# Feed forward input products cut to 256 columns, with twelve kinds of chunk beginnings

## The chip, the cores and the metric

One core of one Trainium2 chip runs the program. The metric is the device time of one execution in microseconds (us); less is better. The time before is the median of three runs.

## What is computed

The reference is a decoder trunk of two layers over 256 positions and a width of 2048, in float32: first a recurrent layer (RG-LRU) with its feed forward part, then a sliding-window attention layer with its feed forward part. The change touches the first half of the two feed forward parts alone:

```python
def swiglu_ffn(x, g, w_in, w_out):
    h = rms_norm(x, g)
    gate, up = jnp.split(h @ w_in, 2, axis=-1)
    return x + (jax.nn.silu(gate) * up) @ w_out
```

Here `x` is 256 x 2048, `w_in` 2048 x 11264 and `w_out` 5632 x 2048. Inputs and outputs are float32.

## The kernel before, in words

**Numbers in two halves.** Every float32 operand is split into a high half (the value rounded to the product format) and a low half (the rest). A product is then high weights by high activations, high weights by low activations, and low weights by high activations. Activations of one tile of 128 features lie side by side in a tile `s` of 512 columns: columns 0 to 255 the high halves of the 256 positions, columns 256 to 511 the low halves. So one matmul of 512 columns with the high weights makes the first two of the three products, and one of 256 columns with the low weights makes the third. The first goes to all 512 columns of a PSUM bank, the second to columns 0 to 255; the two halves of the bank are added when it is drained (`pull`, L341: a copy by ScalarE, an add by VectorE).

**Chunks and groups.** Weights come as 705 jobs of 512 KB, each a chunk of 2 x 128 input features (`kt` or `k`) by 4 x 128 outputs (`f`). `stream` loads a chunk four jobs ahead on SyncE's queue, splits it three jobs ahead (`split`: a copy by ScalarE at L240 into `hi`, a subtraction by VectorE at L241 into `lo`; four buffers each), and then issues its products. A feed forward input group is eight chunks (`group`, with `nk` = 16) that add up into four PSUM banks; two groups take turns with the eight banks. There are 22 groups a layer, 44 in all. A chunk holds eight tiles, and a tile is a pair (k, f).

**What sets the order.** `ffn` gives each group an order, `(None, *self.ORDERS)[g % 8]`: by turns the plain one and the seven of the table `ORDERS`, whose entries are written as (f, k, p), where p is `h` (512 columns of the high weights), `l` (256 columns of the low weights), or `a` and `b` (the two halves of `h`). The plain order goes through `prod` (L272 and L274, one h and one l by turns), the others through `ordered` (L298). The first seven chunks of a group follow its order. The last chunk always goes through `prod`, which turns the pair round for the last k (L268 and L269). In an abl group all products go to columns 0 to 255 of the bank, and the bank is drained by a copy alone (`whole`); its last chunk runs in halves too (L263, L264, L266). Background work (activations, norms, attention) is put between the jobs and at the middle of a job (`half_tick`, `run_bg`) as long as ScalarE and VectorE have room by the estimates that the program keeps.

Of the kernel before, what the change touches and what calls it, by code (L numbers as in the profile page):

```python
# [17 lines left out]
P = 128  # L18
D = 2048
T = 256  # L20
DFF = 5632
ND = D // P
NH = DFF // P
# [25 lines left out]
class Trunk:  # L49
# [208 lines left out]
    def prod(self, ps, hi, lo, c, xs, first, last, one=False):  # L258
# [16 lines left out]

    ORDERS = {
        "hhll": [(f, k, p) for f in range(4) for p in "hl" for k in range(2)],
        "allh": [(f, k, p) for p in "hl" for f in range(4) for k in range(2)],  # L280
        "abl": [(f, k, p) for f in range(4) for k in range(2) for p in "abl"],
        "banks": [(f, k, p) for k in range(2) for p in "hl" for f in range(4)],
        "turns": [(f, k, p) for k in range(2) for f in range(4) for p in "hl"],
        "hllh": [(f, k, p) for f in range(4) for k, p in ((0, "h"), (0, "l"), (1, "l"), (1, "h"))],
        "pairs": [(f, k, p) for k in range(2) for g in range(2) for p in "hl" for f in (2 * g, 2 * g + 1)],
    }

    def ordered(self, order, ps, hi, lo, x2, first):
        mm = self.nc.tensor.matmul
        todo = self.ORDERS[order]  # L290
        begun = set() if first else set(range(4))
        for n, (f, k, p) in enumerate(todo):
            if 2 * n == len(todo):
                self.half_tick()
            w = (lo if p == "l" else hi)[:, k * 512 + f * P:k * 512 + f * P + P]
            c0, c1 = {"h": (0, 2 * T), "l": (0, T), "a": (0, T), "b": (T, 2 * T)}[p]
            o = ps[f][:, 0:c1 - c0]
            mm(o, w, x2[k][:, c0:c1], start=f not in begun, stop=False)  # L298
            begun.add(f)

    def group(self, src, nk, xs, done, last=False, one=False, order=None):

        st = {}
        for c in range(nk // 2):
            def mm(hi, lo, c=c):
                if c == 0:
                    st["ps"] = [self.bank() for _ in range(4)]
                x2 = [self.need(xs[2 * c + kt]) for kt in range(2)]
                if c == nk // 2 - 1:

                    for f in range(4):
                        if f == 2:
                            self.half_tick()
                        for kt in range(2):
                            k = 2 * c + kt
                            self.prod(st["ps"][f], hi, lo, kt * 512 + f * P, x2[kt], False, k == nk - 1, one)
                elif not self.started:
                    self.started = True
                    for kt in range(2):
                        for part in ((hi, None), (None, lo)):  # L320
                            for f in range(4):
                                self.prod(st["ps"][f], *part, kt * 512 + f * P, x2[kt], kt == 0, False, one)
                        if kt == 0:
                            self.half_tick()
                elif order:
                    self.ordered(order, st["ps"], hi, lo, x2, c == 0)
                else:
                    for f in range(4):
                        if f == 2:
                            self.half_tick()  # L330
                        for kt in range(2):
                            k = 2 * c + kt
                            self.prod(st["ps"][f], hi, lo, kt * 512 + f * P, x2[kt], k == 0, False, one)
                if last:
                    for q in x2:
                        self.free(q)
                if c == nk // 2 - 1:
                    done(st["ps"])
            self.jobs.append((src(c), mm))

    def pull(self, ps):  # L341

        t = self.t()
        o = self.half()
        self.a(t, ps[:, T:2 * T])
        self.tt(o, ps[:, 0:T], t, ALU.add)
        self.free_bank(ps)
        return o

    def whole(self, ps):  # L350

        o = self.half()
        self.a(o, ps[:, 0:T])
        self.free_bank(ps)
        return o

# [92 lines left out]
    def ffn(self, l, xs, r, gains, rn, out=None):  # L449
        hid = [Val() for _ in range(NH)]  # L450
        w = self.d[f"ffn_in{l}"]
        for g in range(NH // 2):
            order = (None, *self.ORDERS)[g % 8]

            def done(ps, g=g, one=order == "abl"):
                v = [self.whole(p) if one else self.pull(p) for p in ps]

                def task():
                    while not self.rv[r].ready:
                        yield 1  # L460
                    rs = self.rstd[r][:, 0:T]
                    for h in range(2):
                        ga, up = v[2 * h], v[2 * h + 1]
                        self.tt(ga, ga, rs, ALU.mult)
                        self.a(ga, ga, AF.Silu)
                        self.tt(up, up, rs, ALU.mult)
                        yield
                        self.tt(ga, ga, up, ALU.mult)
                        while not self.slots:
                            yield 1  # L470
                        s = self.slot()
                        self.split_act(s, ga)
                        self.free_half(ga)
                        self.free_half(up)
                        hid[2 * g + h].ap = s
                        hid[2 * g + h].ready = True
                        yield
                self.spawn(task())
            self.group(lambda c, g=g: w[g, c], ND, xs, done, g == NH // 2 - 1, order == "abl", order)
        self.project(self.d[f"ffn_out{l}"], NH, hid, gains, rn, out)  # L480


# [561 lines left out]
```

## Time and profile before

| | |
|---|---|
| median of the three runs | 2039.64 us (2039.63 to 2039.89) |
| the profiled execution | 2040.28 us |
| its span, first to last instruction | 2038.4 us |
| TensorE busy (matmuls) | 2027.7 us, 99% |
| VectorE busy | 1315.1 us, 65% |
| ScalarE busy | 1102.0 us, 54% |
| DMA | 376.10 MB, mean 185 GB/s |
| granted TensorE clock | 1.00 |

The page calls TensorE's matmuls PE and its weight loads PEld, VectorE DVE and ScalarE ACT. Every matmul instruction has a weight load of its own, and the loads run beside the matmuls before them. The ends of matmuls are modelled: one that is shown with 0.28 us is followed by the next some 0.12 us after its start. So the time of a matmul in a run is read from start to start, and where a row merges several of them (x8), its length is that from the first start to the last modelled end.

### The profile page before, as it was taken

What the parts mean: (1) busy time and instruction counts of PE and PEld (TensorE: products, weight loads), DVE (VectorE), ACT (ScalarE), POOL (GpSimd) and SP (SyncE); (2) the same over time, 40 slices, a digit from 0 to 9 for tenths busy, and PEclk for the clock granted to TensorE, in tenths of its full rate; (3) what the DMA queues carried; (4) which work ended last, traced back from release to release, by engine and by line L of the source; (5) the groups of instructions that cost most, each with busy time, mean ns of one, the idle gap of its engine ahead of it and who ended that gap; (6) DMA issues with size and microseconds to landing.
All of it is one profiled execution on the core that took longest, in us unless ns stands there. A gap on an engine that the chain in (4) does not pass through costs nothing.

```text
span 2038.4 us, 32783 instructions
## 1 busy us (share of the span) xinstructions
PE 2027.7 (99%) x12916; PEld 1827.5 (90%) x12916; DVE 1315.1 (65%) x2162; ACT 1102.0 (54%) x1737; POOL 0.2 (0%) x4
## 2 busy tenths in 40 slices
PE   8999999999999999999999999999999999999999
PEld 8999988988998898888898888899889889988899
DVE  8889867566656656545768776765665566554443
ACT  7689656445545544434556775654454454444342
POOL 0000000000000000000000000000000000000000
PEclk9999999999999999999999999999999999999999
DMA  7565555555555555555554335555556556556663
GB/s 258 182 192 182 192 187 186 193 189 186 193 190 189 191 189 187 190 191 186 188 185 145 119 118 167 186 187 191 191 186 196 187 187 195 187 187 200 200 197 125
DMA packets 104987, 376.10 MB, mean 185 GB/s; under 512 B 11648, under 2 KB 13824, under 8 KB 104832
## 3 DMA queue, kind: packets, MB, share of 16 engines
q1 hardware_dynamic: 104832, 374.01, 56.5%
q8 instruction: 101, 1.65, 0.3%
q14 instruction: 54, 0.44, 0.1%
HBM read 371.86 MB, written 2.10 MB: 183 GB/s over the span
## 4 chain that ended last, share of the span: by engine, by line
PE 98%; DVE 1%; DMA 0%; ACT 0%; issue 0%; SPq 0%; DVEq 0%
PE b L298 36%; PE b L272 28%; PE b L274 14%; PE b L264 4%; PE b L266 4%; PE b L263 4%; PE b L269 3%; PE b L268 1%; PE b L863 1%; DMA raw<-in_lru_in 0%; PE b L882 0%; PE b L929 0%; PE b L815 0%; PE b L817 0%; PE b L816 0%; DVE lo L241 0%
## 5 line engine op out<-in xcount | busy, mean ns | idle before, releaser
L241 DVE TENSOR_TENSOR lo<-raw,hi 128x1024 fp32r<-128x1024 f32 (+1 forms) x705 | 861.5, 1222 | 647.9 <-ACT hi L240 644.6
L240 ACT ACTIVATE hi<-raw 128x1024 fp32r<-128x1024 f32 (+1 forms) x705 | 745.3, 1058 | 821.1 <-PE b L272 336.9
L272 PE MATMUL b<-s,hi 128*128 128x512 f32 x2442 | 867.7, 395 | 0.0
L274 PE MATMUL b<-s,lo 128*128 128x256 f32 x2442 | 685.9, 281 | 0.0
L298 PE MATMUL b<-s,hi 128*128 128x512 f32 (+1 forms) x2464 | 655.2, 362 | 0.0
L272 PEld LDWEIGHTS b<-s,hi 128*128 128x128 f32 x2442 | 459.5, 188 | 95.9 <-issue 0.5
L274 PEld LDWEIGHTS b<-s,lo 128*128 128x128 f32 x2442 | 458.2, 188 | 8.9
L298 PE MATMUL b<-s,lo 128*128 128x256 f32 x2128 | 440.9, 279 | 0.0
L298 PEld LDWEIGHTS b<-s,hi 128*128 128x128 f32 x2464 | 403.5, 188 | 32.7
L298 PEld LDWEIGHTS b<-s,lo 128*128 128x128 f32 x2128 | 369.0, 188 | 43.0
L263 PE MATMUL b<-s,hi 128*128 128x256 f32 x800 | 224.9, 281 | 5.8 <-ACT hi L240 5.8
L264 PE MATMUL b<-s,hi 128*128 128x256 f32 x800 | 224.9, 281 | 0.0
L266 PE MATMUL b<-s,lo 128*128 128x256 f32 x800 | 223.6, 281 | 1.2 <-DVE lo L241 1.2
L263 PEld LDWEIGHTS b<-s,hi 128*128 128x128 f32 x800 | 151.5, 189 | 6.2 <-ACT hi L240 6.1
L266 PEld LDWEIGHTS b<-s,lo 128*128 128x128 f32 x800 | 150.2, 189 | 2.2 <-DVE lo L241 2.2
L264 PEld LDWEIGHTS b<-s,hi 128*128 128x128 f32 x800 | 151.5, 189 | 0.0
L104 ACT ACTIVATE t<-b 128x256 f32<-128x256 f32 x230 | 85.0, 380 | 39.4 <-PE b L269 33.5
L269 PE MATMUL b<-s,hi 128*128 128x512 f32 x230 | 90.3, 393 | 0.0
L113 DVE TENSOR_TENSOR h<-h,rstd 128x256 f32<-128x256 f32 x178 | 69.3, 418 | 0.2
L268 PE MATMUL b<-s,lo 128*128 128x256 f32 x230 | 64.2, 279 | 0.0
L113 DVE TENSOR_TENSOR h<-b,t 128x256 f32<-128x256 f32 x154 | 59.0, 417 | 0.2
L268 PEld LDWEIGHTS b<-s,lo 128*128 128x128 f32 x230 | 43.2, 188 | 10.0
(105 smaller groups left out, 993.3 us busy)
## 6 DMA issues: line engine op xcount, KB each, us to landing
raw<-in_ffn_in SPq DMA_DIRECT2D x352, 512.0 KB, 3.4
raw<-in_ffn_out SPq DMA_DIRECT2D x176, 512.0 KB, 3.5
raw<-in_lru_in SPq DMA_DIRECT2D x63, 512.0 KB, 3.9
raw<-in_lru_out SPq DMA_DIRECT2D x32, 512.0 KB, 3.5
raw<-in_w_q SPq DMA_DIRECT2D x32, 512.0 KB, 3.3
raw<-in_w_o SPq DMA_DIRECT2D x32, 512.0 KB, 3.4
raw<-in_gate SPq DMA_DIRECT2D x8, 512.0 KB, 3.5
raw<-in_kv SPq DMA_DIRECT2D x8, 512.0 KB, 3.3
```

Of the source, the lines that this page charges most:

```text
L104: self.nc.scalar.activation(out, in_, func, **kw)
L113: self.nc.vector.tensor_tensor(out, a, b, op)
L240: self.nc.scalar.activation(hi[:, q], raw[:, q], AF.Copy)
L241: self.nc.vector.tensor_tensor(lo[:, q], raw[:, q], hi[:, q].bitcast(F32), ALU.subtract)
L263: mm(ps[:, 0:T], hi[:, c:c + P], xs[:, 0:T], start=first, stop=False)
L264: mm(ps[:, 0:T], hi[:, c:c + P], xs[:, T:2 * T], start=False, stop=False)
L266: mm(ps[:, 0:T], lo[:, c:c + P], xs[:, 0:T], start=False, stop=last)
L268: mm(ps[:, 0:T], lo[:, c:c + P], xs[:, 0:T], start=False, stop=False)
L269: mm(ps[:, :], hi[:, c:c + P], xs[:, :], start=first, stop=True)
L272: mm(ps[:, :], hi[:, c:c + P], xs[:, :], start=first, stop=False)
L274: mm(ps[:, 0:T], lo[:, c:c + P], xs[:, 0:T], start=False, stop=False)
L298: mm(o, w, x2[k][:, c0:c1], start=f not in begun, stop=False)
```

## The change

The table of orders is gone. `ordered` now builds the order of a chunk from a beginning, a short word from the table `BEGIN`, chosen by layer, group and chunk. Each letter of the word takes a product of the next tile: `h` is 512 columns, `w` is columns 0 to 383 and `n` columns 384 to 511 of the tile begun with `w`, and `l` is the low weights of the first tile that has only its `h`. What is left of the chunk is done tile by tile in products of 256 columns (`a`, `b` and `l`; `a` and `b` both have the high weights). The first chunk of a group begins with four `h` and four `l` and does the other four tiles in 256 columns. The last chunk goes through `prod` as before. All groups now work this way, the plain ones too, and all banks have two halves, so `whole` is gone and every bank is drained by `pull`.

```diff
-    ORDERS = {
-        "hhll": [(f, k, p) for f in range(4) for p in "hl" for k in range(2)],
...
-    }
-    def ordered(self, order, ps, hi, lo, x2, first):
+    BEGIN = ["", "h", "hh", "hhh", "hhhh", "hhhhh", "hhhhhh", "hlh", "wn", "hlhh", "w", "hhlhh"]
+
+    def begins(self, l, g, c):
+        return self.BEGIN[(5 * c + 7 * g + 3 * l + g // 3) % len(self.BEGIN)]
+
+    def ordered(self, begin, ps, hi, lo, x2, first):
+
         mm = self.nc.tensor.matmul
...
+        cols = {"h": (0, 4), "a": (0, 2), "b": (2, 4), "l": (0, 2), "w": (0, 3), "n": (3, 4)}
+        tiles = [(k, f) for k in range(2) for f in range(4)]
+        todo, rest, t = [], [], iter(tiles)
+        if first:
+
+            todo = [(k, f, "h") for k, f in tiles[:4]] + [(k, f, "l") for k, f in tiles[:4]]
+            todo += [(k, f, p) for k, f in tiles[4:] for p in "abl"]
+        else:
+            done = {q: "" for q in tiles}
+            for p in begin:
+                if p == "n":
+                    q = next(q for q in tiles if done[q] == "w")
+                elif p == "l":
+                    q = next(q for q in tiles if done[q] == "h")
+                else:
+                    q = next(q for q in tiles if not done[q])
+                done[q] += p
+                todo.append((*q, p))
+            for q in tiles:
+                left = {"": "abl", "h": "l", "w": "nl", "wn": "l", "hl": ""}[done[q]]
+                todo += [(*q, p) for p in left]
...
+            c0, c1 = (P * q for q in cols[p])
+            mm(ps[f][:, c0:c1], w, x2[k][:, c0:c1], start=first and k == 0 and p == "h", stop=False)
...
-            order = (None, *self.ORDERS)[g % 8]
-
-            def done(ps, g=g, one=order == "abl"):
-                v = [self.whole(p) if one else self.pull(p) for p in ps]
+            def done(ps, g=g):
+                v = [self.pull(p) for p in ps]
...
-            self.group(lambda c, g=g: w[g, c], ND, xs, done, g == NH // 2 - 1, order == "abl", order)
+            self.group(lambda c, g=g: w[g, c], ND, xs, done, g == NH // 2 - 1,
+                       begins=lambda c, g=g: self.begins(l, g, c))
```

On TensorE the first feed forward group of layer 0 began like this (in a row: the line, the bank `b` that is written, the activations `s`, the weights `hi` or `lo`, and the columns):

```order
L272 MATMUL b_84<-s_2932,hi_75 128x512
L274 MATMUL b_84<-s_2932,lo_79 128x256
L272 MATMUL b_84<-s_2944,hi_75 128x512
L274 MATMUL b_84<-s_2944,lo_79 128x256
L272 MATMUL b_85<-s_2932,hi_75 128x512
L274 MATMUL b_85<-s_2932,lo_79 128x256
```

Its first chunk now reads as follows; `x2` marks the products `a` and `b` of one tile.

```order
L312 MATMUL b_83<-s_2932,hi_75 128x512
L312 MATMUL b_84<-s_2932,lo_79 128x256
L312 MATMUL b_85<-s_2932,lo_79 128x256
L312 MATMUL b_86<-s_2932,lo_79 128x256
L312 MATMUL b_83<-s_2932,lo_79 128x256
L312 MATMUL b_84<-s_2944,hi_75 128x256 x2
L312 MATMUL b_84<-s_2944,lo_79 128x256
L312 MATMUL b_85<-s_2944,hi_75 128x256 x2
L312 MATMUL b_85<-s_2944,lo_79 128x256
```

The row at the top is the last of four 512-wide products; behind it come sixteen 256-wide ones in a row where wide and narrow products took turns. The third chunk of the same group has the beginning `w`:

```order
L312 MATMUL b_84<-s_3104,hi_77 128x384
L312 MATMUL b_84<-s_3104,hi_77 128x128
L312 MATMUL b_84<-s_3104,lo_81 128x256
L312 MATMUL b_85<-s_3104,hi_77 128x256 x2
L312 MATMUL b_85<-s_3104,lo_81 128x256
```

Here one product of 512 columns became one of 384 and one of 128, and the other seven tiles are in products of 256 columns.

## Rows read from the trace of the kernel before

**Rows 1.** The page: engine totals, and the chain of waits by engine.

```profile
PE 2027.7 (99%) x12916; PEld 1827.5 (90%) x12916; DVE 1315.1 (65%) x2162; ACT 1102.0 (54%) x1737; POOL 0.2 (0%) x4
...
PE 98%; DVE 1%; DMA 0%; ACT 0%; issue 0%; SPq 0%; DVEq 0%
```

**Rows 2.** The page, costliest groups: busy, mean ns of one | idle before.

```profile
L241 DVE TENSOR_TENSOR lo<-raw,hi 128x1024 fp32r<-128x1024 f32 (+1 forms) x705 | 861.5, 1222 | 647.9 <-ACT hi L240 644.6
L240 ACT ACTIVATE hi<-raw 128x1024 fp32r<-128x1024 f32 (+1 forms) x705 | 745.3, 1058 | 821.1 <-PE b L272 336.9
```

**Rows 3.** Stretch of layer 0's input stage: length, PE busy, PEclk, DMA share, GB/s.

```profile
306.08:794.92 488.84, 488.84 (x3011) 1.00 0.58 190
```

**Rows 4.** The chain in layer 0's input stage, groups 1 to 6: start, us.

```profile
328.42 19.32 PE b L298 x112
350.50 19.28 PE b L298 x112
...
372.56 19.79 PE b L298 x168
395.17 19.37 PE b L298 x112
...
417.32 19.53 PE b L298 x112
...
439.65 19.32 PE b L298 x112
```

**Rows 5.** Timeline of TensorE, first chunks of the allh group: start, us, engine.

```profile
350.34 2.00 PE L298 MATMUL b<-s,hi 128*128 128x512 f32 x8
352.18 1.07 PE L298 MATMUL b<-s,lo 128*128 128x256 f32 x8
353.08 1.99 PE L298 MATMUL b<-s,hi 128*128 128x512 f32 x8
354.91 1.11 PE L298 MATMUL b<-s,lo 128*128 128x256 f32 x8
```

**Rows 6.** Two stretches in the projections of the first layer, 256-wide products only.

```profile
26.09:35.04 8.95, 8.95 (x81) 1.00 0.84 265
60.06:69.01 8.95, 8.95 (x79) 1.00 0.54 179
```

**Rows 7.** Timeline of TensorE in the hhll group.

```profile
328.72 0.39 PE L298 MATMUL b<-s,lo 128*128 128x256 f32 x2
328.95 0.62 PE L298 MATMUL b<-s,hi 128*128 128x512 f32 x2
329.40 0.40 PE L298 MATMUL b<-s,lo 128*128 128x256 f32 x2
329.64 0.62 PE L298 MATMUL b<-s,hi 128*128 128x512 f32 x2
```

**Rows 8.** Timeline of TensorE, from the hllh group to the pairs group.

```profile
461.57 0.62 PE L298 MATMUL b<-s,hi 128*128 128x512 f32 x2
462.03 0.39 PE L298 MATMUL b<-s,lo 128*128 128x256 f32 x2
462.25 0.62 PE L298 MATMUL b<-s,hi 128*128 128x512 f32 x2
```

**Rows 9.** Timeline of TensorE, first chunk of the banks group, behind abl.

```profile
395.01 1.09 PE L298 MATMUL b<-s,hi 128*128 128x512 f32 x4
395.94 0.62 PE L298 MATMUL b<-s,lo 128*128 128x256 f32 x4
396.39 1.07 PE L298 MATMUL b<-s,hi 128*128 128x512 f32 x4
397.31 0.63 PE L298 MATMUL b<-s,lo 128*128 128x256 f32 x4
397.78 1.09 PE L298 MATMUL b<-s,hi 128*128 128x512 f32 x4
```

**Rows 10.** The chain in the attention stage: 128-wide products.

```profile
1118.97 0.55 PE b L863 x5
```

More of the change, by code (lines that the diff above doesn't have):

```diff
@@ L274, in prod @@
                 mm(ps[:, 0:T], lo[:, c:c + P], xs[:, 0:T], start=False, stop=False)
-    ORDERS = {
-        "hhll": [(f, k, p) for f in range(4) for p in "hl" for k in range(2)],
[L280 to L285, printed above, removed]
-    }
@@ L288, in ordered @@
-    def ordered(self, order, ps, hi, lo, x2, first):
-        mm = self.nc.tensor.matmul
[L290 to L293, printed above, removed]
+    BEGIN = ["", "h", "hh", "hhh", "hhhh", "hhhhh", "hhhhhh", "hlh", "wn", "hlhh", "w", "hhlhh"]
+    def begins(self, l, g, c):
+        return self.BEGIN[(5 * c + 7 * g + 3 * l + g // 3) % len(self.BEGIN)]
+    def ordered(self, begin, ps, hi, lo, x2, first):
+        mm = self.nc.tensor.matmul
+        cols = {"h": (0, 4), "a": (0, 2), "b": (2, 4), "l": (0, 2), "w": (0, 3), "n": (3, 4)}
[18 more added lines that the diff above has]
+                todo += [(*q, p) for p in left]
+        for n, (k, f, p) in enumerate(todo):
+            if 2 * n == len(todo) - len(todo) % 2:
@@ L294, in ordered @@
                 self.half_tick()
             w = (lo if p == "l" else hi)[:, k * 512 + f * P:k * 512 + f * P + P]
[L296 to L301, printed above, removed]
+            c0, c1 = (P * q for q in cols[p])
+            mm(ps[f][:, c0:c1], w, x2[k][:, c0:c1], start=first and k == 0 and p == "h", stop=False)
@@ L303, in group @@
+    def group(self, src, nk, xs, done, last=False, one=False, begins=None):
         st = {}
@@ L324, in mm @@
                             self.half_tick()
-                elif order:
-                    self.ordered(order, st["ps"], hi, lo, x2, c == 0)
+                elif begins:
+                    self.ordered(begins(c), st["ps"], hi, lo, x2, c == 0)
                 else:
@@ L346, in pull @@
         self.tt(o, ps[:, 0:T], t, ALU.add)
[L347 to L353, printed above, removed]
         self.free_bank(ps)
```

## Prediction

> **What bounds the kernel now.** I read the page's totals first. TensorE is busy for 99% of the span, and the chain of waits that ended last is 98% TensorE [rows 1]. So the time is the sum of the start-to-start distances of the products, and nothing else is worth looking at as long as the other engines stay behind. Weights are split three chunks ahead: a chunk takes about 2.76 us on TensorE (19.32 / 7 [rows 4]), its two split instructions 1.06 us of ScalarE and 1.22 us of VectorE [rows 2].
>
> Next the stage that the change touches, as a stretch: 488.84 us in layer 0, all of it busy and at the full granted clock of 2.4 GHz [rows 3]; layer 1's stage repeats it, so 977.7 us together. Then the chain inside one of them. It merges the seven first chunks of each feed forward input group into one piece, and the six pieces here are the orders hhll, allh, abl, banks, turns and hllh [rows 4]; pairs, the next, repeats hllh's 19.32. All hold the same columns, 56 tiles of one 512-wide and one 256-wide product (in abl three of 256), and yet they take 19.28 to 19.79 us.
>
> The reason shows in the timeline, from start to start. In allh, eight wide products take 1.84 us in one chunk and 1.83 in the next, 0.229 each; but the eight narrow ones, shown from the first start to the modelled end of the last, take 1.07 us in the first chunk and 1.11 in the second [rows 5]. From start to start the first eight take 0.90 us, and 0.04 more makes 0.94 for the others. So **a run of 256-wide products has two paces**, about 0.113 and 0.118 us, called tight and loose from here on. A long run keeps its pace: the 168 of abl stand in 19.79 us, 0.1178 each, without a change [rows 4]. In the first layer's projections 8.95 us hold 81 products in one stretch (two of which began before it), 0.1133 each, and 79 in a later one of the same length and kind of products [rows 6]. So either pace can last for dozens of products; TensorE changes between them at a stall or behind wide products.
>
> Which pace follows can be read off. Behind a tight run, two wide products lead to a loose one and behind that loose run two lead to a tight one: in hhll the pairs of narrow ones alternate 0.23 and 0.24 us [rows 7]. Three behind a tight pair (the last of hllh and two of pairs) give a tight pair, 0.22 us [rows 8]. Four in banks go from loose to tight and from tight to loose, 0.45 and 0.47 us [rows 9], and the first four there follow the long loose run of abl. So of the counts modulo three, one keeps a tight pace, and behind a loose run two or four wide products bring it back.
>
> **The change, part by part.** First the counts, by the code. Outside the last chunk of each group there are 44 x 7 = 308 chunks. Before they hold 5,264 products; now 839 of 512 columns, 47 of 384, 47 of 128 and 5,620 of 256, together 6,553. The last chunks lose 48 products (the abl groups ran them in halves), so TensorE gets 1,241 products more for the same columns.
>
> Before, by [rows 4]: a layer has 22 groups, the eight orders in turn; the plain order alternates as turns does, so I give it the same 19.53. That is 3 x (19.53 + 19.32 + 19.28 + 19.79 + 19.37 + 19.53) + 2 x (19.32 + 19.32) = 427.7 us, for both layers 855.5.
>
> Now, if every narrow product is loose: 839 x 0.229 = 192.1; 5,620 x 0.1178 = 662.0; and 47 pairs of 384 and 128. No row has those widths in this stage. For 384 I take the middle of 0.118 and 0.229, 0.173. For 128 the bounds are 0.059 (half of a 256-wide product) and 0.118; the nearest row is five 128-wide products of the attention stage in 0.55 us, 0.110 [rows 10], and I take that. A pair is then 0.283 (bounds 0.177 and 0.347), all of them 13.3 us (8.3 to 16.3). The sum is 867.4, **+11.9 us**. If every one is tight, 5,620 x 0.1133 = 636.7 gives 842.1, **-13.4 us**. Last chunks: by the starts of the pieces an abl group lasts 395.17 - 372.56 = 22.61 us, so its last chunk 2.82, and an ordinary one 350.50 - 328.42 - 19.32 = 2.76 [rows 4]; six abl ones become ordinary, -0.4 together. So the change costs 11.5 - 25.3 x f, with f the share of narrow products at the tight pace; the break-even is f = 0.45.
>
> **The value of f** is the whole forecast. By the readings above a beginning with wide products ends tight for one of three phases it can come from, and the twelve beginnings with five and seven steps through the table hit the phases evenly; the beginning without wide products keeps what it finds. That is a third. I take 0.30, a little less, because a single wide product has not led to a tight run in any row here, and the beginnings with narrow products in between (hlh, hlhh, hhlhh) and with 384 have no row at all. The bounds are 0.20, if all those without a row go loose, and 0.50, if all go tight.
>
> One term more: behind a loose run four wide products took 0.93 us and behind a tight one 0.92 [rows 9]. With 0.01 us for some 120 chunks that begin with wide products behind a loose run it is +1.2 us (0 if the row's last digit is rounding, 2.4 if every beginning pays it).
>
> Sum: 11.5 - 0.30 x 25.3 + 1.2 = **+5.1 us**. The profiled execution took 2040.28 us, 0.64 more than the median of 2039.64; against the median the forecast is 2044.7 us.
>
> Costed at nothing: the six abl groups are now drained by a copy and an add for each bank, not by a copy alone, so VectorE gets 24 adds of 256 columns. Each is below the 1.22 us of a split of 1024 columns [rows 2], so all are below 29 us of an engine that is busy for 65% of the span [rows 1]. The banks that they free are wanted a whole group, 22 us, later. If VectorE came late, the low halves of the weights would be late next, and TensorE would show gaps at the first low product of a chunk; the lead of three chunks covers that. The queue of weight loads keeps its rows and its order, and a chunk that takes 2.72 to 2.83 us asks for its 512 KB no faster than now.
>
> **The skill against the trace.** The rows give 0.229 us for a wide product and 0.113 or 0.118 for a narrow one, so 15.7 ns above the column time at 2.4 GHz in the first and 6.6 or 11.1 in the second [rows 4, 5, 6]. The Trainium skill, page "TensorE: Matmul & The Clock Gate", section "Back-to-back issue gap", has one formula for a warm array: columns by 2.4 plus about 2.5 ns, whatever came before. It speaks against the change, since each cut would add 2.5 ns: an estimate by that page of 1,241 x 2.5 ns = +3.1 us. The trace does not agree: neither its constants nor a pace that depends on what came before is in that formula.
>
> **Rivals.** (a) *The tight pace never holds here*: at every beginning the narrow products fall to the loose pace, as the whole of abl did [rows 4]. f below 0.1: +9 to +12.7, some 2051 us. For it: the longest narrow runs of this stage are all loose. Against: the 79 tight ones elsewhere [rows 6] and the eight of allh [rows 5].
>
> (b) *Each product has a price of its own* and the pace is only a mean over neighbours, so that the mix decides: hhll gives 19.32 / 56 - 0.229 = 0.116 for a narrow one [rows 4], and the sum is 192.1 + 13.3 + 5,620 x 0.116 - 855.5 - 0.4 = +1.4, 2041.0 us. For it: short runs alternate. Against: abl at 0.1178 with no mix. The skill's formula above is a rule of this kind.
>
> (c) *The tight pace is the rule*, the other side: once won it stays, because chunk boundaries and the short beginnings do not break it, and loose runs are caught by the next long beginning. It is faster than before from f = 0.45, and measurably so from 0.62. At f = 0.65 it is 11.5 - 16.4 + 0.5 = -4.4, 2035.2 us. For it: a tight run of 79 with no help. Against: counts of 1, 2, 4 and 5 behind a tight run, two thirds of the beginnings, end it by the rule above.
>
> (d) *A new wait*: low halves asked for earlier in a chunk, or banks freed late. At 0.06 us in each of 308 chunks it would be +18. Against: TensorE is busy for the whole of that stage [rows 3], and weights lead by three chunks.
>
> **How the numbers follow.** What a measurement of this kernel can tell from no change is about 0.2%, 4.1 us. The forecast's case (f from 0.2 to 0.5) has 0.52, and within it two of three chances lie above +4.1. Rival a has 0.15, b 0.20, c 0.08, d 0.05. Slower: 0.35 + 0.15 + 0.05 + 0.02 of b = 0.57. Within: 0.17 + 0.18 = 0.35. Faster: c, 0.08. The range goes from -1.1 (f = 0.5 with the restarts at nothing) to +10.9 (f near 0.05 with them), 2038.5 to 2050.5; it leaves out c, d and the upper part of a.
>
> **What would show it.** In the timeline after, narrow runs of 10 to 24 at either 0.113 or 0.118 us each, constant within a chunk, with about three in ten at the tight pace; an input stage of about 491.4 us against 488.9 [rows 3]; wide products at 0.229; the 384 and 128 pair near 0.28; no idle time on TensorE. I am wrong if runs change pace inside a chunk, if nearly all are loose or tight, or if gaps appear at a chunk's first low product.

## The result, and the profile after

The changed kernel took 2049.69 us (median of four, 2049.33 to 2050.24) and the kernel before, beside it, 2039.77. The ratio is 1.0047 with a 95% interval of 1.0032 to 1.0063: **9.9 us slower**. Forecast were 5.1 us, within a range that reaches to +10.9.

The page of the profiled execution after (2049.54 us), totals, chain by engine, and the two groups of the changed line:

```profile
PE 2036.8 (99%) x14157; PEld 1886.8 (92%) x14157; DVE 1323.0 (65%) x2186; ACT 1098.4 (54%) x1737; POOL 0.2 (0%) x4
...
PE 98%; DVE 1%; DMA 0%; ACT 0%; issue 0%; SPq 0%; DVEq 0%
...
L312 PE MATMUL b<-s,hi 128*128 128x256 f32 (+2 forms) x4089 | 812.2, 302 | 0.0
...
L312 PE MATMUL b<-s,lo 128*128 128x256 f32 x2464 | 602.6, 280 | 0.0
```

As in [rows 1], TensorE is the whole of it. There are 1,241 matmuls more, as counted, and the new line never has to wait (0.0 at the end of both rows); so the 24 added adds of VectorE and the other order of the weight halves cost nothing.

Stretches after: the two input stages, and the first three output groups of layer 1 behind the second one (length, PE busy, granted clock, DMA share, GB/s):

```profile
304.30:797.82 493.52, 493.52 (x3645) 1.00 0.61 188
1302.19:1795.98 493.79, 493.79 (x3626) 1.00 0.61 188
1795.98:1982.38 186.40, 186.40 (x1057) 1.00 0.62 192
```

Before, the stages took 489.88 and 489.94 us:

```profile
305.03:794.91 489.88, 489.88 (x3015) 1.00 0.58 189
1298.98:1788.92 489.94, 489.94 (x3016) 1.00 0.58 189
```

The stretch that stands at 488.84 us in [rows 3] is not the whole stage: it starts at 306.08, three tiles behind the stage's first product at 305.03. So the two stages came to 979.8 us before, not to 977.7, and the change costs 3.6 and 3.9 us in them. The third row after is a surprise: the change does not touch that line of work, and before it took 184.12 us, 2.3 less:

```profile
1788.92:1973.04 184.12, 184.12 (x1058) 1.00 0.61 194
```

The input stage of layer 0 began 0.7 us earlier than before, and the work between the two input stages took 504.4 us instead of 504.1. So the span's 9.3 us are, up to rounding, 7.5 for the changed stages, 2.3 for untouched work behind them, and -0.4 for untouched work ahead of and between them.

In the timeline the two paces are there. From the first two chunks of the second group that follow its opening one:

```profile
330.35 0.39 PE L312 MATMUL b<-s,hi 128*128 128x256 f32 x2
330.58 0.28 PE L312 MATMUL b<-s,lo 128*128 128x256 f32 x1
330.69 0.39 PE L312 MATMUL b<-s,hi 128*128 128x256 f32 x2
...
333.07 1.30 PE L312 MATMUL b<-s,hi 128*128 128x512 f32 x5
334.21 0.75 PE L312 MATMUL b<-s,lo 128*128 128x256 f32 x5
...
335.04 0.28 PE L312 MATMUL b<-s,lo 128*128 128x256 f32 x1
335.16 0.40 PE L312 MATMUL b<-s,hi 128*128 128x256 f32 x2
335.39 0.28 PE L312 MATMUL b<-s,lo 128*128 128x256 f32 x1
335.51 0.40 PE L312 MATMUL b<-s,hi 128*128 128x256 f32 x2
335.75 0.28 PE L312 MATMUL b<-s,lo 128*128 128x256 f32 x1
335.86 0.40 PE L312 MATMUL b<-s,hi 128*128 128x384 f32 x2
336.10 0.33 PE L312 MATMUL b<-s,lo 128*128 128x256 f32 x1
336.27 0.40 PE L312 MATMUL b<-s,hi 128*128 128x256 f32 x2
```

The first chunk has no wide products and goes on at the tight pace it found: 24 narrow ones from 330.35 to 333.07, 0.1133 each. Five wide ones end that; the three products from 335.16 to 335.51 take 0.35, the loose pace. The chunk that begins with 384 columns, at 335.86, shows the price of that pair: `x2` merges it, 0.24 us, and the narrow product behind it takes 0.17 instead of 0.12.

Counted from the starts of the 5,620 narrow products, 1,269 stand under 0.1155 us to the next: f = 0.23. By chunks, 76 of the 308 end at the tight pace. No chunk's last run of narrow products changes its pace on the way. The words `w` and `wn` turn out to give the same order of products, so the twelve words are eleven orders.

### The profile page after: what moved, and what is told of

Read it like the earlier page. It is cut to its first block, busy times and chain, and to the rows that moved or that the text cites. A ratio compares the mean times of both kernels' runs of the same rounds, so it can differ in the third digit from the quotient of the medians.

```text
span 2047.7 us, 35292 instructions
## 1 busy us (share of the span) xinstructions
PE 2036.8 (99%) x14157; PEld 1886.8 (92%) x14157; DVE 1323.0 (65%) x2186; ACT 1098.4 (54%) x1737; POOL 0.2 (0%) x4
## 4 chain that ended last, share of the span: by engine, by line
PE 98%; DVE 1%; DMA 0%; ACT 0%; issue 0%; SPq 0%; DVEq 0%
PE b L312 42%; PE b L272 24%; PE b L274 12%; PE b L263 4%; PE b L266 4%; PE b L264 4%; PE b L269 3%; PE b L268 1%; PE b L868 1%; PE b L887 0%; PE b L934 0%; PE b L820 0%; DMA raw<-in_lru_in 0%; PE b L822 0%; PE b L821 0%; DVE lo L241 0%
## 5 line engine op out<-in xcount | busy, mean ns | idle before, releaser
L312 PE MATMUL b<-s,hi 128*128 128x256 f32 (+2 forms) x4089 | 812.2, 302 | 0.0
L272 PE MATMUL b<-s,hi 128*128 128x512 f32 x2130 | 761.7, 395 | 0.0
L312 PEld LDWEIGHTS b<-s,hi 128*128 128x128 f32 x4089 | 640.3, 188 | 20.1
L312 PE MATMUL b<-s,lo 128*128 128x256 f32 x2464 | 602.6, 280 | 0.0
L274 PE MATMUL b<-s,lo 128*128 128x256 f32 x2130 | 599.0, 281 | 0.0
L272 PEld LDWEIGHTS b<-s,hi 128*128 128x128 f32 x2130 | 400.5, 188 | 82.4 <-issue 0.5
L263 PE MATMUL b<-s,hi 128*128 128x256 f32 x752 | 211.2, 281 | 6.1 <-ACT hi L240 6.0
L266 PE MATMUL b<-s,lo 128*128 128x256 f32 x752 | 209.6, 280 | 1.2 <-DVE lo L241 1.2
L264 PE MATMUL b<-s,hi 128*128 128x256 f32 x752 | 210.4, 280 | 0.0
L263 PEld LDWEIGHTS b<-s,hi 128*128 128x128 f32 x752 | 142.0, 189 | 6.3 <-ACT hi L240 6.3
L264 PEld LDWEIGHTS b<-s,hi 128*128 128x128 f32 x752 | 141.5, 188 | 0.0
L104 ACT ACTIVATE t<-b 128x256 f32<-128x256 f32 x254 | 94.0, 380 | 39.7 <-PE b L269 34.6
L269 PE MATMUL b<-s,hi 128*128 128x512 f32 x254 | 99.7, 393 | 0.0
L268 PE MATMUL b<-s,lo 128*128 128x256 f32 x254 | 70.8, 279 | 0.0
L113 DVE TENSOR_TENSOR h<-b,t 128x256 f32<-128x256 f32 x178 | 66.7, 417 | 0.1
```

Source lines behind the costliest of these rows:

```text
L104: self.nc.scalar.activation(out, in_, func, **kw)
L113: self.nc.vector.tensor_tensor(out, a, b, op)
L263: mm(ps[:, 0:T], hi[:, c:c + P], xs[:, 0:T], start=first, stop=False)
L264: mm(ps[:, 0:T], hi[:, c:c + P], xs[:, T:2 * T], start=False, stop=False)
L266: mm(ps[:, 0:T], lo[:, c:c + P], xs[:, 0:T], start=False, stop=last)
L268: mm(ps[:, 0:T], lo[:, c:c + P], xs[:, 0:T], start=False, stop=False)
```

## The experiments

Two explanations were set against the theory that the pace is set where a run begins (theory P): that the word at the chunk's beginning decides by itself (theory W; behind the second chunk of a group each word of the changed kernel always follows the same other word, so its profile can't tell), and that a product has one price (theory M). The first four runs changed only the words, and each is a single execution. The 977.7 us for the input stages before, which some expectations give, is the short stretch spoken of above; the stages took 979.8.

**Two wide products everywhere.**

```diff
-        return self.BEGIN[(5 * c + 7 * g + 3 * l + g // 3) % len(self.BEGIN)]
+        return "hh"
```

> Every chunk from the second to the seventh of an input group begins with two 512-wide products and goes on with twenty 256-wide ones. Theory P (the pace of a narrow run is set once, where it begins, by the pace and length of the narrow run before it and by the number of wide products between, and then stays): two wide products lead from a tight run to a loose one and back, so tight and loose chunks take turns, about 175 of the 308 chunks end tight; the two input stages take about 975 us together (changed kernel 987.3, before 977.7), the execution about 2037. Theory W (the word at the chunk's start decides by itself; in the changed kernel 13 of 19 such chunks ended tight): tight and loose in no fixed turn, about two in three tight, 973 us. Theory M (a price per product, 0.1173 us for a narrow one whatever its neighbours, as the mean in the changed kernel): 986 us, the execution about 2048.

The input stages:

```profile
305.30:793.20 487.90, 487.90 (x3703) 1.00 0.61 190
1300.30:1788.23 487.93, 487.93 (x3704) 1.00 0.61 190
```

Together 975.8 us, as expected by theory P; 170 chunks tight. But for the first two groups of each layer the chunks take turns without an exception. The execution took 2041.78 us, not 2037: stretches that nobody changed took 3.0 us more between the input stages (507.1 and not 504.1) and 2.3 more behind them than in the kernel before (below).

**Four everywhere** (`return "hhhh"`).

> Every chunk from the second to the seventh begins with four 512-wide products and goes on with sixteen 256-wide ones. Theory P: four lead from tight to loose and, behind a loose run of sixteen, back to tight, so chunks take turns, about 175 of 308 tight, the two input stages about 975.5 us together, the execution about 2038. Theory W: none of the 22 such chunks of the changed kernel ended tight, so nearly all are loose, about 987 us, the execution 2049. Theory M: 984 us, 2046.

Two chunks of the timeline, TensorE:

```profile
451.93 1.07 PE L312 MATMUL b<-s,hi 128*128 128x512 f32 x4
452.84 0.63 PE L312 MATMUL b<-s,lo 128*128 128x256 f32 x4
453.31 0.40 PE L312 MATMUL b<-s,hi 128*128 128x256 f32 x2
...
454.72 1.09 PE L312 MATMUL b<-s,hi 128*128 128x512 f32 x4
455.65 0.62 PE L312 MATMUL b<-s,lo 128*128 128x256 f32 x4
456.11 0.39 PE L312 MATMUL b<-s,hi 128*128 128x256 f32 x2
...
457.47 0.39 PE L272 MATMUL b<-s,hi 128*128 128x512 f32 x1
```

The first chunk's sixteen narrow products take 1.88 us (452.84 to 454.72), the second's 1.82 (455.65 to 457.47). The word is the same in both, and in the changed kernel it never led to the tight pace; here 130 of 264 chunks with it do. Both input stages come to 975.8 us. So the word does not decide, and theory W is out. The execution took 2040.48 us.

**Three everywhere** (`return "hhh"`).

> Every chunk from the second to the seventh begins with three 512-wide products and goes on with eighteen 256-wide ones. Theory P: three wide products keep a tight pace, so once won it is never lost, nearly all of the 308 chunks are tight, the two input stages take about 963.5 us together and the execution about 2025.5, which is 14 less than before. Theory W: 20 of 24 tight as in the changed kernel, 970.5 us, 2033. Theory M: 985 us, 2047.

```profile
305.08:787.28 482.20, 482.20 (x3571) 1.00 0.61 193
1294.69:1777.00 482.31, 482.31 (x3572) 1.00 0.61 193
```

964.5 us, 15.3 less than before and 23 less than the changed kernel, with 301 of 308 chunks tight. Of the 257 beginnings with three wide products behind a tight run all stayed tight; two more, which have the six products of a norm in front of them, went loose. A single price per product (985 us) is out. The execution took 2030.55 us, beside 2039.82 for the kernel before; theory P had 2025.5, without the stretches between and behind the stages, which took 5.6 us more than in the kernel before here too.

**The same words in another order.**

```diff
-    BEGIN = ["", "h", "hh", "hhh", "hhhh", "hhhhh", "hhhhhh", "hlh", "wn", "hlhh", "w", "hhlhh"]
+    BEGIN = ["w", "hhhhhh", "hhhhh", "hhlhh", "wn", "hlhh", "", "hlh", "h", "hh", "hhhh", "hhh"]
```

> The same twelve words, each about as often as in the changed kernel, but in another order in the table, so that each word follows another one. Theory P: the pace depends on the word before, and with this order about 116 of 308 chunks end tight (76 in the changed kernel); the two input stages take about 983 us together instead of 987.3, the execution about 2045. Theories W and M: the words are the same, so the time is that of the changed kernel within 1 us, and the same share of chunks is tight.

A miss for both: 85 chunks tight, not 116; the input stages 493.29 and 492.63, 985.9 us, so 1.4 less than in the changed kernel and not 4; the execution 2051.77 us, more than the changed kernel. The number 116 rested on guesses of how words with 384 columns or with narrow products inside hand on, and five of the twelve words are of that kind. None of the 107 chunks with those five ended tight. What the other words did still answers the question: four wide products ended tight in 10 of 22 chunks here (0 of 22 in the changed kernel), five in 3 of 19 (0 of 21), an empty beginning in 12 of 24 (3 of 20).

**Where the rest comes from.** In the first four runs the stretch behind layer 1's input stage took what it took after the change. It holds untouched output projections that take wide and narrow products by turns. In these four runs the same four groups of layer 0 went the longer way too. Here they are before, after the change, and with two wide products everywhere:

```profile
794.91:1040.39 245.48, 245.48 (x1409) 1.00 0.58 189
797.82:1043.31 245.49, 245.49 (x1409) 1.00 0.61 189
793.20:1041.72 248.52, 248.52 (x1409) 1.00 0.59 187
```

These 3.0 us are nearly all that the work between the stages took more there. Two runs changed only the last input group of each layer, one in the changed kernel and one in the kernel before:

```diff
-                       begins=lambda c, g=g: self.begins(l, g, c))
+                       begins=None if g == NH // 2 - 1 else lambda c, g=g: self.begins(l, g, c))
```

> The changed kernel, but the last input group of each layer (group 21) goes through the old plain order, one wide and one narrow product by turns, so that the stage ends as it began to end before. Theory P extended to the stages behind (the untouched output projections, which take wide and narrow by turns, also have two paces, 0.3488 and 0.353 us a pair, and keep the one that the end of the input stage hands them): the stretch behind layer 1's input stage falls from 248.5 us in the changed kernel to the 246.2 of before, and the execution takes about 2047.5. Rival: that stretch is longer for another reason (placement, more drains), and stays at 248.5; the execution takes 2049.7.

```diff
-            order = (None, *self.ORDERS)[g % 8]
+            order = (None, *self.ORDERS)[g % 8] if g < NH // 2 - 1 else "hhll"
```

> The kernel before with one edit: the last input group of each layer uses the order hhll instead of turns. Its own seven chunks gain 0.2 us a layer. Theory P extended to the stages behind: the output projections of layer 1 are handed another phase and can fall to the looser alternation, 248.5 us behind the stage instead of 246.2, so the execution takes about 2041.7, longer than before. Rival: nothing behind the stage changes, 2039.4.

The same three output groups, in the changed kernel with its last group by turns:

```profile
1796.60:1980.72 184.12, 184.12 (x1057) 1.00 0.63 195
```

and in the kernel before with its last group in hhll:

```profile
1788.45:1972.57 184.12, 184.12 (x1058) 1.00 0.61 195
```

The first, a single execution like the second, did what was expected: 2.3 us come back, and the execution took 2047.86. The second did not: hhll hands on the shorter alternation just as turns does, and the execution took 2039.73, as the rival had it. So how an input stage ends does set the pace of the untouched stage behind it, but which ends lead to which pace I can't say in advance. The stretch has 528 pairs of one wide and one narrow product: 0.3487 us each at 184.12, 0.3530 at 186.40.

**A kernel made for the tight pace.** If three wide products keep it, all the two-half groups should be written that way. The core of the edit:

```diff
+    def ordered(self, odd, ps, hi, lo, x2, first, last):
...
+        word = "0h 1h 2h 0l 1l 3h 4h 5h 2l 3l 4l 5l 6a 6b 6l 7a 7b 7l"
+        if odd:
+            word = "0a 0b 0l 1a 2h 3h 4h 1b 1l 2l 3l 4l 5a 5b 5l 6a 6b 6l 7a 7b 7l"
...
-            self.group(lambda c, g=g: w[g, c], ND, xs, done, g == NH // 2 - 1,
-                       begins=lambda c, g=g: self.begins(l, g, c))
+            self.group(lambda c, g=g: w[g, c], ND, xs, done, g == NH // 2 - 1)
```

The digit is the tile of the chunk; even and odd chunks take turns, and the order is used for both layers' input and output projections, the recurrent output, the queries and the attention output.

> Every two-half group of the kernel (input and output projections, recurrent output, queries, attention output) runs chunks in which wide products come three at a time, each three followed by 2, 14 or 14 narrow products (a number that leaves 2 over by three), last chunks too. Theory P: from any state two or three such beginnings lead to the tight pace, and three wide products keep it, so every chunk takes about 2.731 us: 961 us for the two input stages (before 977.7, changed kernel 987.3), about 5 us less in each output projection, and some 2007 us in all (2000 to 2015; attention work between the products can break the pace). Theory M: 0.1173 us for a narrow one gives 2.79 us a chunk, no gain in the input stages, and an execution of about 2040.

The input stage of layer 0, the output projections behind it, and the input stage of layer 1:

```profile
302.42:783.87 481.45, 481.45 (x3441) 1.00 0.62 193
783.87:1024.11 240.24, 240.24 (x1719) 1.00 0.63 193
1280.11:1761.51 481.40, 481.40 (x3441) 1.00 0.63 193
```

The 88 output chunks take 2.730 us each, as expected; the two input stages 962.8 us. The execution took **2006.36 us**, a ratio to the kernel before of 0.9833 (0.9818 to 0.9847).

**The same, and one group for the recurrent stage.**

```diff
-            self.group(lambda c: w[4 + g, c], ND, xs, done, one=True)
+            self.group(lambda c: w[4 + g, c], ND, xs, done, one=g != 2)
```

(and that group's banks are drained by a copy and an add)

> The same, and the third group of the recurrent layer's projections is run and drained in two halves in that order too. Theory P: the 256-wide products of the recurrent stage behind it, all loose before at 0.1178 us, are handed the tight pace and keep it for some 1,300 products, 0.0045 us each: about 6 us less than the kernel with threes elsewhere, some 2001 us. Rival: the longer drain or the gates break the pace again, and the time stays at that of the other kernel.

Two stretches of its recurrent stage, 256-wide products only:

```profile
78.35:180.00 101.65, 101.65 (x899) 1.00 0.62 189
190.00:210.00 20.00, 20.00 (x172) 1.00 0.63 192
```

Behind the group with wide products 896 products start in 101.65 us, 0.113 each (the row counts three that began before). From about 185 us on the pace is loose again (170 start in 20 us):

```profile
184.88 0.28 PE L264 MATMUL b<-s,hi 128*128 128x256 f32 x1
184.99 0.28 PE L266 MATMUL b<-s,lo 128*128 128x256 f32 x1
185.22 0.39 PE L263 MATMUL b<-s,hi 128*128 128x256 f32 x1
185.44 0.28 PE L264 MATMUL b<-s,hi 128*128 128x256 f32 x1
185.56 0.28 PE L266 MATMUL b<-s,lo 128*128 128x256 f32 x1
```

Two products there are 0.23 and 0.22 us from the next start, and behind them the run is loose. What held them up was not looked into. The execution took **2001.22 us**, 5.1 less than without this edit, and a ratio to the kernel before of 0.9807 (0.9791 to 0.9824). The kernel before had a median of 2040.55 in that series, so this is 39.3 us less, and 48.5 less than the changed kernel.

## Why the prediction was right, and where it was not

**The mechanism was right.** Narrow products have two paces, a run keeps the one it begins with, and wide products between runs set it. In the changed kernel and the four runs that changed only its words, behind a tight run one, two, four and five wide products led to a loose run (3, 130, 134 and 18 of as many), and three and six kept it tight (267 and 5 of as many). Four more such beginnings have a norm's six products in front of them, and all four ended loose, two with three wide products among them.

Behind a loose run the same word goes both ways. What decides there was worked out after the result, from the starts in the traces, as a count by threes: each wide product adds one, each narrow product of a loose run adds one, those of a tight run add nothing, and a run of two or more is tight when the count stands at a multiple of three where it begins. In the three kernels with one word everywhere this gives the pace of 912 of 924 chunks, with the count at the start of a layer chosen to fit; the other twelve stand behind a norm's products or in the first chunk of the group after. For mixed words it is not complete: with the steps of the five words that have 384 columns or narrow products inside fitted to both profiles, it gives 273 of 308 chunks in the changed kernel and 239 in the reordered one, where calling every chunk loose gives 232 and 223.

**The step that failed is f**, "the twelve beginnings with five and seven steps through the table hit the phases evenly". They don't. With a step of five in a table of twelve, each word follows one and the same other word, but for the edges of groups. Four and five wide products always came where they lead to a loose run (0 of 43), and one never led to a tight run; two, three and six mostly did (50 of 67). Together the words of wide products alone give 50 of 134 chunks, so the third of the prediction holds for them in the mean. What is missing from f is mostly elsewhere: of the five words that had no row not one of 110 chunks ended tight, which the prediction had as its lower bound of 0.20, and the beginning without wide products ended tight in 3 of 20. So f was 0.23 and not 0.30; by 25.3 us for all narrow products that is 1.8 us. Running the rule through the table would have shown the fixed neighbours, but hardly the number: for the reordered table that gave 116 chunks, and 85 came.

**The terms of the sum.** The sum gave the two stages +5.1 us, and they took 7.5 more (987.3 against 979.8). The first seven chunks took 863.6 us by the starts in the trace, without the norm's six products in each layer (0.8 us a layer, before and after), where the sum (867.4 - 7.6 + 1.2) had 861.0. Of the 2.6 us 1.8 is f; the wide products, at 0.2307 us on average and not 0.229, took 1.5 more than priced, of which the term for restarts had allowed 1.2; the rest is not traced to a term. The pair of 384 and 128 columns was sized by the middle and a row of another stage at 0.283. It measured 0.231 with 0.052 more for the product behind it, the same sum in another place. The chunks before were priced well, at 855.5 for 855.8 without the norms. So were the last chunks: -0.4 forecast, and 122.1 us for the 44 against 122.4 before. The 977.7 us of the prediction is the short stretch of [rows 3]; the sum does not rest on it, but the sign to look for, 491.4 against 488.9, does, and measured were 493.5 against 489.9. By the sum the range's +10.9 belongs to an f of 0.07, not of 0.05.

**What was costed at nothing and was not**: the stages behind. The sum stopped at the border of the input stage, because the untouched products there are the same before and after. They are, but they too have two paces, 0.3487 and 0.3530 us a pair, and the changed kernel hands those of layer 1 the longer one: 2.3 us. The last-group run shows it, since it gives them back. Those of layer 0 kept the shorter pace in this change; in the four runs with other words they lost it, 3.0 us more.

**The time alone would not have told.** The 9.9 us lie in the stated range, near its end of +10.9, and rival (a) had +9 to +12.7. That the range held is in part luck, as the 2.3 us of the stages behind are in no term of it. The mechanism rests on the two paces in the timeline and on f, which at 0.23 is within the bounds of 0.20 and 0.50.

The Trainium skill's formula (page "TensorE: Matmul & The Clock Gate", section "Back-to-back issue gap"), a warm matmul at its columns by 2.4 plus about 2.5 ns, which the page gives as the gap of an isolated matmul, made +3.1 us as an estimate here. What the runs show is not of that form. The page of the profile of the last kernel has 14,603 matmuls,

```profile
PE 1989.1 (99%) x14603; PEld 1865.5 (93%) x14603; DVE 1319.2 (66%) x2190; ACT 1094.4 (55%) x1741; POOL 0.2 (0%) x4
```

where the kernel before has 12,916 [rows 1]; by the formula's fixed part alone that is an estimate of +4.2 us, and it takes 39.3 us less.

Of the rivals, (a) is out by f, 0.23 and not below 0.1, with 76 chunks that end tight, (b) by the kernel with three wide products, and (d) by the idle time of 0.0 at the changed line. Rival (c), the tight pace as the rule, did not happen in this change, but it is what three wide products at a time make of it.

**What stays open** is why three. The starts in the traces repeat by threes as well: wide products in a row stand 226, 229 and 232 ns apart by turns, tight ones 113, 113 and 114, loose ones 118, 118 and 117. But the runs show the rule and its prices, not what in the chip counts. Open too is how words with 384 columns or single narrow products inside hand the pace on.

## What to carry to other kernels

When TensorE is never idle, read its products from start to start, by runs of equal width: the same instruction can come at two paces, and an order of the same work can be worth nearly 2%. A rule for what follows what has to be run through the actual order, to the end of the program; a mean over all cases hides both the fixed predecessors of a table and the stages behind, which keep the pace they are handed. And a stretch that is compared before and after has to begin at the same product in both. In this stream of 512- and 256-wide float32 products, wide ones three at a time with 2 or 14 narrow ones behind them took about 2.73 us a chunk in both input stages and in the output projections behind the first.

## What was not expected of the hardware

- A run of 256-wide products goes on at 0.1133 or 0.1178 us for as long as nothing comes between (896 products in 101.65 us, 24 without a wide product in 2.72), under the same granted clock of 1.00, and the state goes through chunk borders and from one stage to the next.
- The choice goes by three: three or six wide products keep the tight pace (272 of 272), one, two, four and five end it (285 of 285), where nothing else stands between.
- Wide and narrow by turns also have two paces, 0.3487 and 0.3530 us a pair, for a whole stage.
- A 128-wide product behind a 384-wide one took about 0.06 us to the next start, and the 256-wide one behind it 0.17 instead of 0.118 (means of 47 in the changed kernel).
